# A hybrid decoder layer on one core: a third place for row tiles, one cast on VectorE, and other priorities for the scheduler

## The chip, the core and the metric

The kernel runs on one core of a Trainium2 chip. The metric is the device time in microseconds (us) of one execution; lower is better. The core has TensorE (matmul), VectorE, ScalarE and GpSimd (named DVE, ACT and POOL in the profile), and SyncE (SP), which here only issues DMA transfers.

## What is computed

One layer of a decoder on 2048 rows (positions) of width 1024, all in float32. Shapes: 8 heads of 64 with 2 key/value heads and a window of 128; the other half of the mixer is a gated convolution over three positions; the feed-forward width is 4096.

```python
def reference(x, attn_norm_g, w_in, q_norm_g, k_norm_g, sinks, conv_w,
              attn_out_g, conv_out_g, w_out, mlp_norm_g, w_up, w_down):
    for l in range(DEPTH):                      # DEPTH = 1
        h = rms_norm(x, attn_norm_g[l])
        z = h @ w_in[l]
        ...                                     # q, k, v, gate_b, gate_c, xc are columns of z
        q = rms_norm(q, q_norm_g[l])
        k = rms_norm(k, k_norm_g[l])
        y_attn = swa_sink_attention(q, k, v, sinks[l])
        y_conv = gate_b * short_conv(gate_c * xc, conv_w[l])
        y = jnp.concatenate([rms_norm(y_attn, attn_out_g[l]),
                             rms_norm(y_conv, conv_out_g[l])], axis=-1)
        x = x + y @ w_out[l]
        hm = rms_norm(x, mlp_norm_g[l])
        x = x + jnp.square(jax.nn.relu(hm @ w_up[l])) @ w_down[l]
    return x
```

## The kernel before

**Precision.** A float32 product is made of three matmuls: each operand is split into a high part (a cast on ScalarE) and a low part (value minus high part, on VectorE), and `mm3` (L271) adds high x high, high x low and low x high into one PSUM bank. Lines 273, 274 and 275 are these three.

**Stages.** The mixer part (to about 690 us) works through four chunks of 512 rows. The feed-forward part follows: the up product (`u`, L1430) and the down product (`d`, L1537), each in seven block products in Strassen's manner, with x rows and weights combined ahead of time.

**The first chunk** (`first_chunk`, L489, called L595) is issued by hand, in program order on every engine. Its first product goes through eight slices k of the width: `load_x0` and `load_w0` fetch them, `turn(k)` transposes the x slice on TensorE (`pt_a`), `split0(k)` splits the weights (`w_q`), `moved(k)` multiplies the transposed slice by the norm's gain and splits it into high and low (`h_a`, L515 and L516), and `product0(k)` runs 12 matmuls into four banks (`pz`). `spin(n)` issues matmuls of the identity whose result nobody reads, to have TensorE at work while the first data come in; `SPIN` holds two numbers of them. ScalarE's first work on data is the cast of `w_q` for k = 0 and then `h_a` for k = 0.

**The later order** is made by a scheduler that places the instructions of each engine by priority. Two generators are interleaved in each chunk. `mixers` (L1007) goes through the four blocks of 128 rows of the attention: scores (`psc`), softmax (`sc`), probabilities transposed (`ptp`), split into `pp` and masked on GpSimd (L734), the product with the values (`po`, L773), the result `o` on VectorE, the mean of its squares (`pa`, L794, a matmul with `mean`; `ms` is read from it by VectorE). `besides` (L963) yields the big matmuls one step at a time: the convolution's projections (`pc`, `px`, `pb`), the out projection (`pout`, with weights `w_wo` that come back from DRAM in two halves, high and low), the next chunk's rows (`xt_a`, scaled on VectorE in L289, transposed on TensorE) and the next chunk's projection (`pz`). Between the steps of the attention `fill(n)` takes n steps from `besides`; the numbers come from the table `FILL`, a row for each chunk. `ahead(i)` (L195) raises or lowers the priority of a step by column i of the table `PRIO`, a row for each chunk:

```python
def ahead(i):
    offset = PRIO[stage[0]][i]
    return tc.high_priority(offset=offset) if offset else nullcontext()
```

The columns: 0 q and k transposed, 1 softmax, 2 q and k normed, 3 `pa`, 4 values and probabilities, 5 `po`, 6 attention output, 7 split of weights, 8 scaling of rows, 9 transposes of rows, 10 convolution, 11 eviction of the out projection. `LATER` lowers the priority of writing split weights to DRAM.

**The end of chunk 3.** `prepare_mlp` (L929) prepares x for the up product. Eight row tiles (t, i) of 128 rows are fetched from DRAM (`xt_m`, `fetch`, L938), scaled on VectorE (L289), and transposed on TensorE in two groups of four (`raised`, L309, `pt_m`), which ScalarE copies into `xm`. Tiles with i = 0 are then written to DRAM (`x_put`, L340, `xop`); those with i = 1 also go through four subtractions on VectorE (`x_sums`, L354) and five writes. There are two places for fetched tiles, so a fetch on SP's queue waits until the tile two before it is transposed. All transposes of row tiles and `pa` go through one PSUM bank (`tr`). SP issues transfers in order: what stands behind a fetch that waits also waits. `xm` are two buffers that take the space of the chunk's `h` (high and low).

## Time and profile before

| what | value |
|---|---|
| three runs | 1925.79, 1926.3, 1927.85 us; median 1926.3 |
| the profiled execution | 1926.52 us, of which the span 1924.7 |
| TensorE | busy 1912.8 us (99% of the span), 8923 instructions |
| VectorE, ScalarE, GpSimd | busy 63%, 43%, 14% |
| chain that ended last | TensorE 90%, VectorE 6%, DMA 2%, issue 1% |
| DMA | 414.32 MB, 215 GB/s on average |

A busy time is the sum of the spans of an engine's instructions. Matmuls overlap, and their ends are modelled, so a TensorE that is busy is not yet one at its peak; the time from start to start of consecutive matmuls says more than their durations. An idle time is put down to what ended last before the instruction could start.

### The profile page before, as it was taken

The page shows a single profiled execution, that of the slowest core. Times are in us where ns is not written, and L with a number is a line of the kernel's source. Part 1 is how long each engine was busy: PE and PEld are TensorE (multiplying, and loading weights), DVE is VectorE, ACT ScalarE, POOL GpSimd, SP SyncE. Part 2 cuts the span into 40 slices and gives each one's busy share as a digit, 9 for nine tenths or more (in the row PEclk, how much of TensorE's full clock was granted, in tenths as well). Part 3 has the DMA queues.
Part 4 walks back from the last instruction along what each step waited for, and adds up shares of the span by engine and source line. Part 5 has one row for each costly group of instructions (what it writes and reads, how often), then busy time and mean ns, then how long its engine had stood idle before and what let it go on. Part 6 is the DMA issues. An engine that isn't in the chain of part 4 may idle for free.

```text
span 1924.7 us, 24566 instructions
## 1 busy us (share of the span) xinstructions
PE 1912.8 (99%) x8923; PEld 1589.3 (83%) x8923; DVE 1204.5 (63%) x1848; ACT 829.9 (43%) x1565; POOL 273.4 (14%) x477
## 2 busy tenths in 40 slices
PE   9999999999999999999999999999999999999999
PEld 8888888888888778888888888888888888888887
DVE  4885657447456769989887767666534334457531
ACT  5564434335344437454565555553432232232320
POOL 2122212302221112223110110101000000100000
PEclk9999999999999999999999999999999999999999
DMA  8984854463573797777665454437954457766631
GB/s 296 335 304 129 316 208 175 189 249 153 190 268 144 257 355 257 220 235 241 218 225 199 168 170 135 161 137 301 373 203 150 142 164 230 278 223 220 212 128 55
DMA packets 232792, 414.32 MB, mean 215 GB/s; under 512 B 51672, under 2 KB 136160, under 8 KB 219872
## 3 DMA queue, kind: packets, MB, share of 16 engines
q1 hardware_dynamic: 203840, 336.98, 51.9%
q0 software_dynamic: 15424, 51.40, 6.8%
q10 hardware_dynamic: 13408, 24.39, 3.4%
q8 instruction: 70, 1.15, 0.2%
q14 instruction: 50, 0.41, 0.1%
HBM read 286.87 MB, written 125.83 MB: 214 GB/s over the span
## 4 chain that ended last, share of the span: by engine, by line
PE 90%; DVE 6%; DMA 2%; issue 1%; ACT 1%; POOL 1%; ACTq 0%; SPq 0%; DVEq 0%; POOLq 0%
PE d L1537 32%; PE u L1430 29%; PE pout L273 3%; PE pout L275 3%; PE pout L274 3%; PE pz L273 2%; PE pz L274 2%; PE pz L275 2%; PE pc_c L273 1%; PE pc_c L275 1%; PE pc_c L274 1%; PE psc_b L685 1%; PE pz L523 1%; PE px_c L274 1%; PE px_c L273 1%; PE px_c L275 1%
## 5 line engine op out<-in xcount | busy, mean ns | idle before, releaser
L1430 PE MATMUL u<-op_x,wop 128*128 128x512 f32 x2688 | 610.3, 390 | 0.5 <-DVE wop L424 0.5
L1537 PE MATMUL d<-op_w,op_f 128*128 128x512 f32 x2688 | 609.4, 389 | 0.0
L1430 PEld LDWEIGHTS u<-op_x,wop 128*128 128x128 f32 x2688 | 504.5, 188 | 105.8 <-DVE wop L424 0.9
L1537 PEld LDWEIGHTS d<-op_w,op_f 128*128 128x128 f32 x2688 | 504.7, 188 | 104.6
L405 DVE TENSOR_TENSOR op_f<-op_f 128x1024 fp32r<-128x1024 f32 x112 | 136.9, 1224 | 232.4 <-ACT op_f L404 231.9
L404 ACT CAST op_f<-op_f 128x1024 fp32r<-128x1024 f32 x112 | 117.7, 1052 | 352.0 <-DMA op_f<-fop 344.9
L424 DVE TENSOR_TENSOR wop<-wu,wop 128x512 fp32r<-128x512 f32 x156 | 111.8, 718 | 35.0 <-DMA wu<-in_w_up_dram 17.6
L423 ACT CAST wop<-wu 128x512 fp32r<-128x512 f32 x156 | 95.9, 619 | 83.0 <-PE u L1430 79.1
L1166 POOL DMA_DIRECT2D fop<-s x96 | 51.9, 541 | 442.4 <-DVE s L1169 438.1
L1172 DVE TENSOR_TENSOR u<-u,u 128x512 f32<-128x512 f32 x128 | 87.7, 685 | 21.7 <-PE u L1430 21.7
L405 DVE TENSOR_TENSOR op_w<-raw,op_w 128x1024 fp32r<-128x1024 f32 x56 | 68.4, 1222 | 27.2 <-ACT op_w L404 27.0
L404 ACT CAST op_w<-raw 128x1024 fp32r<-128x1024 f32 x56 | 58.8, 1052 | 46.0 <-PE d L1537 23.4
L1178 ACT ACTIVATE u<-u 128x512 f32<-128x512 f32 x64 | 40.5, 633 | 73.1 <-DVE u L1172 71.2
L702 ACT ACTIVATE sc_b<-sc_b,ngm_b 128x128 f32<-128x128 f32 x128 | 49.6, 390 | 23.9 <-DVE ngm_b L699 23.9
L734 POOL TENSOR_SCALAR_AFFINE_SELECT pp_b<-pp_b 128x512 fp32r<-128x512 f32 x60 | 39.6, 673 | 112.6 <-ACT pp_b L727 59.8
L1379 POOL DMA_DIRECT2D wds<-raw x16 | 8.5, 534 | 327.8 <-DVE raw L1377 327.8
L423 ACT CAST wop<-wu_s 128x512 fp32r<-128x512 f32 x64 | 39.6, 620 | 31.0 <-PE u L1430 22.8
L273 PE MATMUL pout<-w_wo,yt_c 128*128 128x512 f32 x128 | 52.5, 410 | 0.0
L275 PE MATMUL pout<-w_wo,yt_c 128*128 128x512 f32 x128 | 52.1, 407 | 0.0
L424 DVE TENSOR_TENSOR wop<-wu_s,wop 128x512 fp32r<-128x512 f32 x64 | 44.6, 698 | 10.9 <-ACT wop L423 10.7
L274 PE MATMUL pout<-w_wo,yt_c 128*128 128x512 f32 x128 | 51.3, 400 | 0.0
L273 PE MATMUL pout<-w_wo,at_b 128*128 128x512 f32 x128 | 50.2, 395 | 0.0
(258 smaller groups left out, 3110.1 us busy)
## 6 DMA issues: line engine op xcount, KB each, us to landing
op_f<-fop SPq DMA_DIRECT2D x112, 512.0 KB, 4.3
raw<-in_w_down_dram SPq DMA_DIRECT2D x72, 512.0 KB, 4.3
wu<-in_w_up_dram SPq DMA_DIRECT2D x128, 256.0 KB, 4.0
w_wo<-wo SPq DMA_DIRECT2D x24, 1024.0 KB, 6.7
fop<-s POOLq DMA_DIRECT2D x96, 256.0 KB, 2.5
fop<-u ACTq DMA_DIRECT2D x64, 256.0 KB, 2.8
op_x<-xop SPq DMA_DIRECT2D x28, 512.0 KB, 6.7
w_q<-q SPq DMA_DIRECT2D x12, 1024.0 KB, 7.5
```

Of the source, the lines that this page charges most:

```text
L273: nc.tensor.matmul(ps, st(0), mv(0), start=first, stop=False)
L274: nc.tensor.matmul(ps, st(0), mv(1), start=False, stop=False)
L275: nc.tensor.matmul(ps, st(1), mv(0), start=False, stop=last)
L404: nc.scalar.copy(op[:, 0], raw)
L405: nc.vector.tensor_tensor(op[:, 1], raw, op[:, 0].bitcast(F32), op=ALU.subtract)
L423: splits.append(nc.scalar.copy(hi, blk).ins)
L424: nc.vector.tensor_tensor(lo, blk, hi.bitcast(F32), op=ALU.subtract)
L702: nc.scalar.activation(sc[:, hd, :], sc[:, hd, :], AF.Exp, bias=ngm[:, hd : hd + 1], accum_out=den[:, hd : hd + 1])
L1166: eng.dma_start(fop_dram[tb][ORDER_DOWN.index(i)][n // 2][:, n % 2], b)
L1172: return nc.vector.tensor_tensor(dst, ps, b, op=ALU.add).ins
L1430: nc.tensor.matmul(pt, wops[i][:, a, k, :], xops[tb, p][k // 2][:, b, k % 2, :], start=p not in GOES_ON and k + j == 0, stop=k + j == NB + ...
L1537: nc.tensor.matmul(ps[tb][j], fs[tb][:, a, k, j * P : (j + 1) * P], w[:, b, k, :], start=first and p not in GOES_ON and k + n == 0, stop=l ...
```

## The change

Four edits. The first product takes the high part of `h` for k = 0 from VectorE and no longer from ScalarE; one more idle matmul is issued behind the first transposes, and the second slice is transposed behind the first four products and no longer ahead of them. In `prepare_mlp` three tiles are fetched ahead; the third and sixth of them go into half of the second `xm` buffer (pieces 3 and 7), which is not in use until later. The tables `PRIO` and `FILL` get other numbers, and `LATER` falls from 250 to 190.

```diff
-SPIN = (5, 0)
+SPIN = (5, 1)
...
-    (40, 0, 160, -10, 10, 0, 10, 60, -20, 30, 0, 300),
+    (40, 0, 160, -10, 30, 0, 10, -10, -20, 30, 0, 300),
...
-    ((27, 6), (9, 9, 5, 6, 3), (6, 7, 8, 5, 5), (8, 13, 8, 7, 7), (10, 1, 9, 5, 0)),
+    ((27, 6), (9, 9, 5, 6, 3), (6, 7, 7, 5, 5), (8, 13, 8, 7, 7), (11, 1, 9, 3, 0)),
...
-                r = slice((NB * k + j) * P, (NB * k + j + 1) * P)
-                nc.tensor.transpose(pt[:, j * P : (j + 1) * P], xt[:, r], ident)
+                r = slice(j * P, (j + 1) * P)
+                nc.tensor.transpose(pt[:, r], xt[:, k, r], ident)
...
-            nc.scalar.activation(h[0][:, k], pt, AF.Copy, scale=g_in[k])
+            if k:
+                nc.scalar.activation(h[0][:, k], pt, AF.Copy, scale=g_in[k])
+            else:
+                nc.vector.tensor_scalar(h[0][:, k], pt, g_in[k], None, op0=ALU.mult)
...
         spin(SPIN[1])
-        turn(1)
...
-            split0(k)
-            moved(k)
+            if k:
+                split0(k)
+                moved(k)
+            else:
+                nc.scalar.copy(hl0[0][:, 0], by_k(raw0[0])[:, 0])
+                moved(0)
+                nc.vector.tensor_tensor(hl0[0][:, 1], by_k(raw0[0])[:, 0], hl0[0][:, 0].bitcast(F32), op=ALU.subtract)
...
-                product0(k, [(i, t) for i in range(3) for t in range(NT)])
+                for i in range(3):
+                    product0(k, [(i, t) for t in range(NT)])
+                    if not k and not i:
+                        turn(1)
...
-            def fetch(t, i):
+            halves = lambda w: w.rearrange("p (k c) -> p k c", k=2)
+
+            def fetch(n):
+                t, i = tiles[n]
                 r = i * CH + t * P
-                xts[t, i] = row("xt", f"xt_m{i}_{t}", 2)
-                nc.sync.dma_start(xts[t, i], x1_dram[r : r + P, :])
+                xt = xs[1][:, 3::4] if n % 3 == 2 else halves(row("xt", f"xt_m{i}_{t}", 2))
+                nc.sync.dma_start(xt, halves(x1_dram[r : r + P, :]))
                 with ahead(8):
-                    scaled(xts[t, i], rs_x1[:, r // P : r // P + 1], gb)
+                    scaled(xt, rs_x1[:, r // P : r // P + 1], halves(gb))
+                xts[t, i] = xt
...
-            fetch(*tiles[0])
-            fetch(*tiles[1])
+            for n in range(3):
+                fetch(n)
...
-                if n + 2 < len(tiles):
-                    fetch(*tiles[n + 2])
+                if n + 3 < len(tiles):
+                    fetch(n + 3)
```

In the tables the other changes are: `PRIO`, chunk 0: values and probabilities 10 to 30, split of weights 60 to -10 (the row shown); chunk 1: scaling of rows 50 to -40; chunk 2: attention output 260 to 120, eviction 10 to 0; chunk 3: `pa` -10 to 200. `FILL`: chunk 0, last block, one step less (5 to 4) ahead of the values; chunk 2, three fewer and one fewer; chunk 3 as shown.

What this does to the order, at three places. First VectorE at the start of the kernel, before and then after (`w_q_0` the weights of slice 0, `h_a_250` the high part of h, `h_a_251` the low part):

```order
L552 COPY g_in<-pg 128x8
L506 TENSOR_TENSOR w_q_0_242<-raw_q_240,w_q_0_242 128x512
L516 SCALAR_TENSOR_TENSOR h_a_251<-pt_a_0_290,g_in,h_a_250 128x512
L506 TENSOR_TENSOR w_q_1_243<-raw_q_240,w_q_1_243 128x512
L516 SCALAR_TENSOR_TENSOR h_a_251<-pt_a_1_295,g_in,h_a_250 128x512
```

```order
L555 COPY g_in<-pg 128x8
L518 TENSOR_SCALAR h_a_250<-pt_a_0_290,g_in 128x512
L519 SCALAR_TENSOR_TENSOR h_a_251<-pt_a_0_290,g_in,h_a_250 128x512
L566 TENSOR_TENSOR w_q_0_242<-raw_q_240,w_q_0_242 128x512
L506 TENSOR_TENSOR w_q_1_243<-raw_q_240,w_q_1_243 128x512
L519 SCALAR_TENSOR_TENSOR h_a_251<-pt_a_1_308,g_in,h_a_250 128x512
```

VectorE has one operation more, and the low part of h now stands ahead of the low part of the weights.

Second GpSimd in chunk 0, around the masking of the probabilities of block 1 (`pp_b_0` and `pp_b_1` are its two head groups; `ms_c` and `rc` the scale of the convolution's half, `ss_a` and `rs_a` that of a row tile of the next chunk), before and then after:

```order
L734 AFFINE_SELECT pp_b_0_1_1484<-pp_b_0_0_1483 128x512
L190 TENSOR_SCALAR ms_c_1536<-ms_c_1536 128x4
L191 TENSOR_TENSOR rc_659<-ms_c_1536,mhalf 128x4
L1000 TENSOR_TENSOR rc_659<-rc_659,rs_252 128x4
L190 TENSOR_SCALAR ss_a_2_1552<-ss_a_2_1552 128x1
L191 TENSOR_TENSOR rs_a_2_1554<-ss_a_2_1552,mhalf 128x1
L734 AFFINE_SELECT pp_b_0_1_1484<-pp_b_0_0_1483 128x512
L734 AFFINE_SELECT pp_b_1_1_1495<-pp_b_1_0_1494 128x512 x2
```

```order
L744 AFFINE_SELECT pp_b_0_1_1485<-pp_b_0_0_1484 128x512 x2
L190 TENSOR_SCALAR ms_c_1537<-ms_c_1537 128x4
L191 TENSOR_TENSOR rc_660<-ms_c_1537,mhalf 128x4
L1014 TENSOR_TENSOR rc_660<-rc_660,rs_252 128x4
L744 AFFINE_SELECT pp_b_1_1_1496<-pp_b_1_0_1495 128x512 x2
L190 TENSOR_SCALAR ss_a_2_1553<-ss_a_2_1553 128x1
```

Both masks of the first group now come ahead of the scale `rc`, and those of the second group ahead of `rs_a`.

Third SP's queue near the end of chunk 3 (`w_wo_0`, `w_wo_1` with 1662 or 1663 as their source are the high and low half of the weights of the last projection piece of the convolution's half; `xt_m` and `xm_6234` are fetches of row tiles), before and then after:

```order
L244 DMA w_wo_0_6453<-wo_0_1662 128x2048
L244 DMA w_wo_1_6454<-wo_1_1663 128x2048
L938 DMA xt_m_2_6266<-x_dram 128x1024
L340 DMA xop_0_76<-xm_6232 256x1x256
L340 DMA xop_1_77<-xm_6232 256x1x256
L938 DMA xt_m_3_6324<-x_dram 128x1024
```

```order
L951 DMA xm_6234<-x_dram 128x2x512
L244 DMA w_wo_0_6455<-wo_0_1663 128x2048
L951 DMA xt_m_3_6269<-x_dram 128x1024
L340 DMA xop_0_76<-xm_6233 256x1x256
L340 DMA xop_1_77<-xm_6233 256x1x256
L340 DMA xop_0_76<-xm_6233 256x1x256
L951 DMA xt_m_0_6327<-x_dram 128x1024
L340 DMA xop_1_77<-xm_6233 256x1x256
L340 DMA xop_0_76<-xm_6233 256x1x256
L951 DMA xm_6234<-x_dram 128x2x512
L340 DMA xop_1_77<-xm_6233 256x1x256
L340 DMA xop_0_76<-xm_6233 256x1x256
```

The third tile's fetch moved ahead of the weights' high half, and the low half (`w_wo_1`, row 176 of the queue before) is no longer behind the high half: it stands in row 189, after the fetches of tiles 3 to 6 as well. The first operand of the up product (`op_x`, L403) moved from row 189 to row 208, behind most writes of the last tile. On TensorE, in chunk 2, 42 rows stand between the last matmul of `po` of block 11 and its `pa` before, and 66 after.

## The prediction

> **What bounds the kernel now.** I read the page first, then what TensorE waits for, then the timeline around each wait.

> ```profile
> PE 1912.8 (99%) x8923; PEld 1589.3 (83%) x8923; DVE 1204.5 (63%) x1848; ACT 829.9 (43%) x1565; POOL 273.4 (14%) x477
> L1430 PE MATMUL u<-op_x,wop 128*128 128x512 f32 x2688 | 610.3, 390 | 0.5 <-DVE wop L424 0.5
> L1537 PE MATMUL d<-op_w,op_f 128*128 128x512 f32 x2688 | 609.4, 389 | 0.0
> ```

> TensorE is busy for 99% of 1924.7 us, and the 5376 matmuls of the two feed-forward products, 63% of the span, wait 0.5 us in all. 609.4 us over 2688 is 0.227 us a matmul (each lasts 0.39 us, but they overlap): that is the pace against which I measure holes. The change removes no matmul, so it can only win holes, and only ahead of 690 us. The view of waits, on TensorE alone, lists them:

> ```profile
> PE idle L547 <- POOL ident L170: 1.6, 1, 1.6
> PE po_b L773 <- POOL pp_b L734: 1.4, 3, 0.9
> PE pt_m L315 <- DVE xt_m L289: 1.4, 2, 1.1
> PE pa_b L794 <- DVE o_b L789: 0.8, 1, 0.8
> PE pt_m L315 <- DVE ms_b L796: 0.6, 1, 0.6
> PE u L1430 <- DVE wop L424: 0.5, 1, 0.5
> PE pz L523 <- ACT h_a L515: 0.4, 1, 0.4
> PE pt_a L511 <- DMA x<-in_x_dram: 0.2, 1, 0.2
> ```

> These eight, the largest, come to 6.9 us. The first is the launch and the sixth lies in the feed-forward part; neither is touched. So about 4.8 us of idle time can go. A hole costs a little more than its idle time, because TensorE's overlap has to start again; below I take start to start, less 0.23.

> **Part 1, the start** (h's high part on VectorE, one more idle product, four transposes moved behind the first four products). The timeline of before:

> ```profile
> 4.22 1.11 PE L511 MATMUL pt_a<-ident,x 128*128 128x128 f32 x4
> 5.57 1.12 PE L511 MATMUL pt_a<-ident,x 128*128 128x128 f32 x4 [0.24 <-DMA x<-in_x_dram]
> 5.86 0.62 ACT L505 CAST w_q<-raw_q 128x512 fp32r<-128x512 f32 x1 [2.52 <-DMA raw_q<-in_w_in_dram]
> 6.38 0.68 ACT L515 ACTIVATE h_a<-pt_a,g_in 128x512 fp32r<-128x512 f32 x1
> 6.51 0.69 DVE L506 TENSOR_TENSOR w_q<-raw_q,w_q 128x512 fp32r<-128x512 f32 x1 [2.02 <-ACT w_q L505]
> 7.11 4.88 PE L523 MATMUL pz<-w_q,h_a 128*128 128x512 f32 x12 [0.42 <-ACT h_a L515]
> 7.11 0.75 DVE L516 SCALAR_TENSOR_TENSOR h_a<-pt_a,g_in,h_a 128x512 fp32r<-128x512 f32 x1
> 11.84 0.60 PE L511 MATMUL pt_a<-ident,x 128*128 128x128 f32 x4
> ```

> ScalarE casts w (to 6.48) and then h (to 7.06), and the first product waits for both. No row shows VectorE writing h's high part; its neighbours there took 0.69 and 0.75. It can begin when the first transposes end, 5.33, so it is done by 6.1, and w becomes last: the first product starts near 6.53 instead of 7.11, 0.58 earlier. VectorE's h low then ends at 6.85 and w low at 7.6, ahead of the fifth product (6.53 + 4 x 0.43 = 8.2). But the second group of transposes, which stood in TensorE's wait, now stands in its stream: four took 1.12 here, some 0.9 of it before the next can start. 0.9 - 0.58 is +0.3; against it, products that start earlier have more of their dozen done when the clock rises. Bounds: -0.6 (the transposes cost nothing) and +0.9 (nothing won by the earlier start). I take **+0.1**. The extra idle product lies in a wait and costs nothing.

> How slow the start is, the rate shows:

> ```profile
> 7.10:8.90 1.80, 1.79 (x4) 1.00 1.04 389
> 11.84:14.60 2.76, 2.57 (x12) 1.00 0.96 342
> ```

> Four of 512 columns start in the first 1.8 us, 0.43 us apiece, yet the granted clock (after the counts) reads 1.00; the first twelve took 11.84 - 7.11 = 4.73 us, the next twelve 2.76 with their transposes. So the array is at half pace until about 11. [...]

> **Part 2, chunk 0** (values and probabilities earlier).

> ```profile
> 130.82 0.68 DVE L728 TENSOR_TENSOR pp_b<-ptp_b,pp_b 128x512 fp32r<-128x512 f32 x1
> 131.08 1.04 POOL L191 TENSOR_TENSOR rc<-ms_c,mhalf 128x4 f32<-128x4 f32 x1
> 132.72 0.40 PE L773 MATMUL po_b<-pp_b,vd 128*128 128x512 f32 x1
> 133.33 1.93 POOL L734 TENSOR_SCALAR_AFFINE_SELECT pp_b<-pp_b 128x512 fp32r<-128x512 f32 x3
> 134.02 0.50 PE L773 MATMUL po_b<-pp_b,vd 128*128 128x512 f32 x1 [0.90 <-POOL pp_b L734]
> ```

> The hole is 134.02 - 132.72 - 0.23 = 1.07 us: GpSimd masks the second half of head group 0 only at 133.33, after the chain for rc. In the new order VectorE splits both groups and GpSimd masks group 0 before that chain and group 1 behind it. I put the last mask, two of 0.64 (a third of 1.93) behind a chain that ends near 131.8, at 133.1 and TensorE's need at 133.6: the hole goes, with 0.5 us to spare. What pays: VectorE does those splits and other steps of 0.7 earlier, ahead of the scaling of the next chunk's first row tile, whose transposes then wait some 0.3 longer, while those of a later tile wait some 0.2 less. Bounds -1.4 (all holes here go) and +0.4 (two steps of 0.7 in front, hole gone). I take **-1.0**. Chunk 1 changes only a few rows, with one scaling later, close to its need: +0.1, between -0.4 and +0.5.

> **Part 3, chunk 2.**

> ```profile
> 539.39 0.39 PE L275 MATMUL pout<-w_wo,at_b 128*128 128x512 f32 x1
> 540.13 0.29 DVE L789 TENSOR_TENSOR o_b<-o_b 128x128 f32<-128x128 f32 x1
> 540.56 0.35 PE L794 MATMUL pa_b<-mean,o_b 128*128 128x1 f32 x2 [0.79 <-DVE o_b L789]
> ```

> A hole of 540.56 - 539.39 - 0.23 = 0.94 us: the mean of the squares of block 11 waits for VectorE. By the new order po_b11 moves up, and 66 matmuls instead of 42 stand between it and pa_b11, 24 more of 256 columns, by half of 0.23 about 2.7 us. VectorE needs the same time as before, so **-0.94**; ends -1.0 and 0 (its own queue is delayed as much).

> **Part 4, chunk 3** (the third place for x rows).

> ```profile
> 638.51 0.80 SPq L244 DMA_DIRECT2D w_wo<-wo  x2
> 661.55 1.28 DVE L289 SCALAR_TENSOR_TENSOR xt_m<-xt_m,rs_x,g_mlp 128x1024 f32<-128x1024 f32 x1 [1.15 <-DMA xt_m<-x_dram]
> 662.98 0.63 PE L315 MATMUL pt_m<-ident,xt_m 128*128 128x128 f32 x4 [1.09 <-DVE xt_m L289]
> 675.80 1.28 DVE L728 TENSOR_TENSOR pp_b<-ptp_b,pp_b 128x512 fp32r<-128x512 f32 x2
> 675.94 0.66 PE L315 MATMUL pt_m<-ident,xt_m 128*128 128x128 f32 x4 [0.60 <-DVE ms_b L796]
> 677.51 0.51 PE L773 MATMUL po_b<-pp_b,vd 128*128 128x512 f32 x1 [0.21 <-POOL pp_b L734]
> 679.25 0.50 PE L773 MATMUL po_b<-pp_b,vd 128*128 128x512 f32 x1 [0.33 <-POOL pp_b L734]
> DMA to landing us min/median/max: 4.7/6.7/8.5
> DMA to landing us min/median/max: 3.2/4.4/8.1
> ```

> (The last two rows are those of w_wo's loads in this window, and of xt_m.) A row tile is fetched only when the transposes of the tile two before it are done; landing (4.4) and scaling (1.28) then decide. With three places the fetch comes one tile earlier. The waits on xt_m (1.4 idle), on ms_b (0.6) and on pp_b (0.54), five holes, go as holes: 2.5 idle plus some 0.17 each to restart is 3.4. Three things take part of it back. First, SP: the low half of the weights of the last projection piece (w_wo, second of the pair at 638.51) moves from in front of all fetches to behind five of them, each waiting for transposes; I follow the order to an issue at about 655 and, with 6.7, a landing at 662, where TensorE wants it at 661 to 661.5: +0.5 to 1. Second, block 15's probabilities stay behind the sums of the row tiles on VectorE, and one bank holds all these transposes: +0.6. Third, the first operand of the up product is now loaded behind the last tile's sums instead of at 658: its split (VectorE, two of 1.22, then 0.7) can end up to 1 us behind TensorE. Together I take +1.5 of 3.4, **-1.9**; ends -4 (nothing new waits) and +1 (all three at their worst, 4.4).

> Sum: 0.1 - 1.0 + 0.1 - 0.94 - 1.9 = -3.64. The profiled run took 1926.52 us (1.8 outside its span), 0.22 above the median, so 1922.9 for it and **1922.6** in terms of the median. A difference of 0.2%, 3.85 us, is about what a measurement can tell from none; the forecast falls just short of it, and its own range, 1920.6 to 1924.6, holds both.

> **Rivals.**
> (a) Everything clears. Part 4 gives -4 and part 2 -1.4, the rest as above: 0.1 - 1.4 + 0.1 - 0.94 - 4 = -6.1, 1920.2. For it: the three repayments each hang on less than 1 us. Against: SP issues in order, and five fetches are ahead of the weights.
> [...]
> (c) Chunk 3 gains nothing, since what was gained on row tiles is waited for on weights and operand: 0 instead of -1.9, 1924.5.
> (d) Slower: the weights' low half lands too late. Every fetch ahead of it on SP waits for a place, so one slow landing (8.1, shown above) at the second and fifth tile shifts it by 3.7 each; with 8.5 for its own, 1.8 more, it lands 9.2 late. TensorE then stands at the projection, since its stream has nothing else in front; the first repayment of 0.5 to 1 becomes 9.7, behind which the others hide: some 8 more, and -3.6 + 8 is +4.4, 1930.7. It decides from a landing near 669.5, where the sum is +3.85. For it: 0.91 of the DMA engines' time is used in this stretch:

> ```profile
> 638.00:690.00 52.00, 49.42 (x258) 38.87 (x257) 39.87 (x64) 22.86 (x41) 9.70 (x14) 1.00 0.91 290
> ```

> Against it: two of eight or more landings would both have to be the worst.

> **How the numbers follow.** Chances: forecast 0.48 (half of it beyond 0.2%), (a) 0.2, (b) 0.08, (c) 0.12, (d) 0.12. Faster is 0.24 + 0.2, and a little of (c) where the other parts do better: 0.46. Slower is (d) and the worst ends of (b) and (c): 0.15. Same is 0.39. The range of 8 in 10 runs from (a) less a start that wins 0.6, 1919.3, to the near end of (d), 1928.5, with the most of (d) left out above.

> **What would show it.** Right: no wait of po_b on pp_b near 133, none of pa_b near 540, first product at 6.5 and the third group of transposes near 11.9; no wait of pt_m on xt_m, and w_wo's last load issued at 655 and landed at 662; u starting near 686.5, all of it shifted by the same amount from there to the end. Wrong: a wait of pout on a DMA of over 2 us after 660, the first twelve products taking 7 us, or new holes in chunk 1.

## The result, and the profile after

| | before | changed |
|---|---|---|
| first comparison, 22 runs each | 1926.6 us median (1924.02 to 1928.76) | 1923.53 (1920.87 to 1927.77) |
| second, 27 and 11 runs | 1927.26 (1924.16 to 1931.43) | 1923.83 (1921.52 to 1925.87) |

The ratio is 0.9983 with a 95% interval of 0.9977 to 0.999, and 0.9985 (0.9976 to 0.9994) in the second: 3.1 to 3.4 us faster, just short of the 0.2% named in the prediction. Forecast were 1922.6 and -3.64.

What TensorE waits for in the changed kernel (engine, line, releaser; total, times, longest):

```profile
PE pout L274 <- DMA w_wo<-wo: 2.2, 2, 1.9
PE idle L550 <- POOL ident L170: 1.6, 1, 1.6
PE po_b L783 <- POOL pp_b L744: 0.7, 1, 0.7
PE pz L526 <- ACT w_q L564: 0.5, 1, 0.5
PE pa_b L804 <- DVE o_b L799: 0.3, 1, 0.3
```

The waits on the row tiles (`xt_m`, 1.4) and on `pa`'s reader `ms_b` (0.6) are gone; those on `pp_b` and `o_b` are down to half or less and stand in other places (675 and 622 us, where it was 134 and 540); at the head stands a wait that was not there, of the last projection piece on its weights. The time by stages, from the starts of TensorE's matmuls in the timeline of two profiles of each kernel (the second of each was taken among the experiments):

| stage, from start to start | before | before again | changed | changed again |
|---|---|---|---|---|
| launch to the last of the 96 first products | 33.60 | 31.22 | 33.19 | 33.77 |
| chunk 0, to the 96th matmul of its out projection | 120.53 | 121.80 | 118.76 | 118.75 |
| to the 145th matmul of chunk 1's out projection | 222.06 | 222.06 | 221.96 | 222.04 |
| over chunk 2, to the first `pb` matmul of chunk 3 | 208.47 | 208.47 | 207.66 | 207.70 |
| to the up product's first matmul | 105.43 | 105.02 | 107.47 | 105.39 |
| up product, its first 1344 matmuls | 316.29 | 315.52 | 316.35 | 316.29 |

(Where an expectation below counts from the last convolution product of chunk 3, it is this `pb` matmul.) Chunk 2 gives 0.8 and chunk 0 gives 1.8 or 3.1; chunk 3, forecast at -1.9, loses 0 to 2.4. In chunk 0 the hole of 1.07 on `pp_b` was the largest; the changed kernel at that place (`ssc` is the sum of squares of the convolution's half, from which `rc` is made):

```profile
125.25 0.68 DVE L875 TENSOR_TENSOR ssc<-ssc,y_c 128x512 f32<-128x512 f32 x1
129.57 1.38 POOL L191 TENSOR_TENSOR rc<-ms_c,mhalf 128x4 f32<-128x4 f32 x1
131.18 1.23 POOL L744 TENSOR_SCALAR_AFFINE_SELECT pp_b<-pp_b 128x512 fp32r<-128x512 f32 x2
132.61 0.71 PE L783 MATMUL po_b<-pp_b,vd 128*128 128x512 f32 x2
```

The last two masks are done at 132.41, before TensorE wants them at 132.61. The timeline of TensorE at the end of chunk 3 in the changed kernel:

```profile
658.32 0.47 PE L273 MATMUL pout<-w_wo,yt_c 128*128 128x512 f32 x1
658.80 0.66 PE L315 MATMUL pt_m<-ident,xt_m 128*128 128x128 f32 x4
659.21 0.71 PE L783 MATMUL po_b<-pp_b,vz 128*128 128x512 f32 x2
661.84 0.55 PE L274 MATMUL pout<-w_wo,yt_c 128*128 128x512 f32 x1 [1.92 <-DMA w_wo<-wo]
662.18 0.63 PE L275 MATMUL pout<-w_wo,yt_c 128*128 128x512 f32 x1
662.61 0.63 PE L273 MATMUL pout<-w_wo,yt_c 128*128 128x512 f32 x1
...
665.17 0.58 PE L273 MATMUL pout<-w_wo,yt_c 128*128 128x512 f32 x1
665.59 0.39 PE L274 MATMUL pout<-w_wo,yt_c 128*128 128x512 f32 x1
665.82 0.39 PE L275 MATMUL pout<-w_wo,yt_c 128*128 128x512 f32 x1
```

L274 is the first product that needs the weights' low half. It waits 1.92, a hole of 661.84 - 659.52 - 0.23 = 2.09 (the second `po_b` started at 659.52). Behind it nine products start 0.43 apart instead of 0.23, until 665.6. The windows of the same stretch (length, busy and count, granted clock, DMA share, GB/s) show why:

```profile
659.80:661.80 2.00, 0.12 (x1) 1.00 0.97 347
661.80:665.40 3.60, 3.56 (x9) 0.55 1.08 375
665.40:669.00 3.60, 3.60 (x16) 0.98 0.21 74
```

Over the 3.6 us behind the hole the granted clock reads 0.55. The hole cost 2.09, and the slow clock behind it some 1.7 more. The load itself, on SP's queue:

```profile
636.82 0.59 SPq L244 DMA_DIRECT2D w_wo<-wo  x1
...
652.23 0.41 SPq L951 DMA_DIRECT2D xt_m<-x_dram  x1
652.85 0.51 SPq L340 DMA_DIRECT2D xop<-xm  x1
653.41 0.60 SPq L244 DMA_DIRECT2D w_wo<-wo  x1
```

The high half is issued at 636.82, the low half at 653.41, and the traced landing is at 661.80, 8.4 us later.

### The profile page after: what moved, and what is told of

The parts are those of the page before. It is cut to its first block, busy times and chain, and to the rows that moved or that the text cites. A ratio compares the mean times of both kernels' runs of the same rounds, so it can differ in the third digit from the quotient of the medians.

```text
span 1923.8 us, 24574 instructions
## 1 busy us (share of the span) xinstructions
PE 1913.5 (99%) x8925; PEld 1591.4 (83%) x8925; DVE 1206.1 (63%) x1849; ACT 830.6 (43%) x1564; POOL 275.8 (14%) x477
## 3 DMA queue, kind: packets, MB, share of 16 engines
q8 instruction: 70, 1.15, 0.2%
## 4 chain that ended last, share of the span: by engine, by line
PE 65%; DMA 1%; SPq 0%; POOL 0%; DVE 0%; ACT 0%; issue 0%; POOLq 0%
PE d L1551 32%; PE u L1444 31%; DMA w_wo<-wo 1%; PE pout L274 1%; PE pout L275 1%; PE pout L273 0%; PE pt_m L315 0%; SPq L244 0%; PE po_b L783 0%; POOL pp_b L744 0%; DVE d L1497 0%; ACT xm L316 0%; SPq L340 0%; SPq L418 0%; PE pa_b L804 0%
## 5 line engine op out<-in xcount | busy, mean ns | idle before, releaser
L1551 PE MATMUL d<-op_w,op_f 128*128 128x512 f32 x2688 | 609.4, 389 | 0.0
L424 DVE TENSOR_TENSOR wop<-wu,wop 128x512 fp32r<-128x512 f32 x156 | 111.5, 716 | 36.2 <-ACT wop L423 18.4
L274 PE MATMUL pout<-w_wo,yt_c 128*128 128x512 f32 x128 | 51.5, 402 | 1.9 <-DMA w_wo<-wo 1.9
L275 PE MATMUL pout<-w_wo,yt_c 128*128 128x512 f32 x128 | 52.5, 410 | 0.0
L424 DVE TENSOR_TENSOR wop<-wu_s,wop 128x512 fp32r<-128x512 f32 x64 | 44.5, 697 | 11.0 <-ACT wop L423 10.8
```

The lines of the kernel that those rows point to most:

```text
L274: nc.tensor.matmul(ps, st(0), mv(1), start=False, stop=False)
L275: nc.tensor.matmul(ps, st(1), mv(0), start=False, stop=last)
L424: nc.vector.tensor_tensor(lo, blk, hi.bitcast(F32), op=ALU.subtract)
L1551: nc.tensor.matmul(ps[tb][j], fs[tb][:, a, k, j * P : (j + 1) * P], w[:, b, k, :], start=first and p not in GOES_ON and k + n == 0, stop=l ...
```

## The experiments

Theory 1: the third place itself gains in chunk 3, and the weights' low half, which it pushes behind the fetches, takes it back. Theory 2: the third place crowds the end of chunk 3 whatever the weights do. Stages are those of the table.

**again**: the changed kernel unaltered.

> The changed kernel as it is, for a second profile and times beside the next two. If the loss at the end of chunk 3 belongs to the order of SP's queue, the wait of the last projection piece for the low half of its weights comes again (1 to 3 us, its load issued near 653 and landing near 660 to 663), and about 3.5 us of products at half pace behind it whenever the wait is near 2 us. If it was an accident of one run, there is no such wait here. Total 1921 to 1926.

The weights were issued at 653.98 and landed at 662.01; the wait came again, with a hole of 1.29, and the clock did not fall. The first profile's half pace is not in every run; the wait is in all six profiles with this order of SP (holes of 1.3 to 2.1, the load taking 8.0 to 8.5 each time).

**weights_early**: the weights of that piece raised in priority.

```diff
-                hl = ahead_parts.pop((half, dh), None) or out_weights(c, half, dh)
+                with tc.high_priority(offset=400) if half and dh and c + 1 == NCHUNK else nullcontext():
+                    hl = ahead_parts.pop((half, dh), None) or out_weights(c, half, dh)
```

> The changed kernel, with only the load of the last projection piece's weights (half 1, second column half, chunk 3) raised in priority, so that both halves stand on SP ahead of the third tile's fetch, as in the kernel before. Theory 1, the weights behind five fetches are the cost: no wait of pout on w_wo after 650, no half pace there, the up product starts 3 to 4 us earlier than in the changed kernel's first profile (near 685.5 instead of 689.0), time 1919 to 1921, that is 2 to 4 below the changed kernel. Theory 2, the third place itself crowds the end of chunk 3 (fetches, one PSUM bank, VectorE): the wait goes, others come, the up product starts at 688 to 689.5 and the time is that of the changed kernel within 1 us.

SP's queue and TensorE's waits (largest three):

```profile
636.67 0.80 SPq L244 DMA_DIRECT2D w_wo<-wo  x2
637.51 0.56 SPq L952 DMA_DIRECT2D xm<-x_dram  x1
```

```profile
PE idle L550 <- POOL ident L170: 1.6, 1, 1.6
PE u L1445 <- DVE wop L424: 0.8, 1, 0.8
PE pz L526 <- DVE h_a L518: 0.5, 1, 0.5
```

Both halves land by 643.91, the wait on w_wo and the half pace are gone. The stage to the up product takes 103.75 us, 1.6 and 3.7 below the two profiles of the changed kernel and 1.3 to 1.7 below the kernel before. In its place stands the wait of `u` on its operands, a hole of 0.97. Theory 1 holds by the stages. The total is 1922.88 (ratio to before 0.9983, 0.9974 to 0.9991) beside 1923.83 in the same comparison: 1 us lower, which the intervals do not separate; the expected 2 to 4 did not show in it.

**early_again** is the same kernel later, beside early_spin3 below.

> The kernel with early weights and one idle product again, beside the one with three: runs spread over 1919.5 to 1926, median near 1922.5; no wait of pout on w_wo near 660; from the last convolution product of chunk 3 (its first matmul) to the first of the up product 103.5 to 104.3 us, against 105.44 in the kernel before and 107.47 and 105.39 in the two profiles of the changed kernel.

The stage took 103.68. Median 1921.92, ratio 0.9981 (0.9972 to 0.999). Here the start of the up product gave back more: a hole of 0.81 on its operands and one of 1.28 for the next weights, 317.88 for its first 1344 matmuls against 316.3.

**no_third**: two places, everything else new.

```diff
-            for n in range(3):
-                fetch(n)
+            fetch(*tiles[0])
+            fetch(*tiles[1])
```

(and the rest of `prepare_mlp` and `raised` as before.)

> The changed kernel with two places for row tiles, as before; start, priorities and filling steps are the new ones. Theory 1: chunks 0 to 2 gain their 3 us as in the changed kernel; chunk 3 has the waits on xt_m, ms_b and pp_b of the kernel before again (about 3.4 us of holes), no wait on w_wo, so the up product starts near 687 and the time is 1922.5 to 1924, about that of the changed kernel. Theory 2: it is faster than the changed kernel by 2 us or more.

```profile
PE pt_m L315 <- DVE xt_m L289: 2.6, 3, 1.8
PE idle L550 <- POOL ident L170: 1.6, 1, 1.6
PE pout L273 <- DMA w_wo<-wo: 0.8, 1, 0.8
```

(The wait on `w_wo` here is one for the next weights, at 690.8 us.) The waits on the row tiles are back, larger than before (a hole of 1.93), and the stage takes 106.46; its median is 1926.03, 2.2 above the changed kernel in the same comparison, 2.0 above the upper end that theory 1 expected, and the contrary of theory 2. By the stage the third place gains nothing sure with late weights (105.4 to 107.5 in the two profiles, against 106.46 without it) and 2.7 with early ones; the stages do not explain the 2.2 of the medians. The stage is also 1.0 to 1.4 longer than in the kernel before, which has two places as well: the new numbers for chunk 3 (`pa` and the filling steps) cost that much by themselves in this profile.

**third_alone**: the kernel before with the third place only.

> The kernel before with the third place alone. Both theories: the start and chunks 0 to 2 stand as before (first product at 7.1, hole at 133, hole at 540). Theory 1: the load of the weights' low half moves behind five fetches here too (so the order says), with a wait of 1 to 3 us; the up product starts between 689 and 692.

As expected in chunk 3 (the start was at full pace, with the first product at 6.72): weights issued at 655.27, landed at 663.61, a hole of 1.99, nine products at half pace, the up product at 690.51; one run of 1927.32. The order of SP comes from the third place and not from the tables.

**undo_p4** and **undo_p7_fill** take back two parts of the tables each.

```diff
-    (40, 0, 160, -10, 30, 0, 10, -10, -20, 30, 0, 300),
+    (40, 0, 160, -10, 10, 0, 10, -10, -20, 30, 0, 300),
...
-    (200, 0, 10, -50, 40, 0, 120, -20, 70, 280, 200, 0),
+    (200, 0, 10, -50, 40, 0, 260, -20, 70, 280, 200, 0),
```

> The changed kernel with two priorities back at their old values: chunk 0, values and probabilities (30 to 10), and chunk 2, attention output (120 to 260). The order of GpSimd in chunk 0 stays new (both masks of the first group ahead of rc, those of the second behind it), but the transposes of the probabilities go back among the projection's products. If the order on GpSimd removed the hole near 132, there is no hole of po_b on pp_b there (under 0.3 us); if it was the earlier transposes and splits, a hole of 0.5 to 1.1 us comes back. Chunk 2: no hole near 540, since the number of matmuls between po_b11 and pa_b11 (67) stays.

No hole near 130, chunk 0 in 118.89 against 118.76: the early transposes, which stand among the projection's products again here, are worth nothing that can be seen. No hole of `pa` near 540; one run of 1924.01.

```diff
-    (40, 0, 160, -10, 30, 0, 10, -10, -20, 30, 0, 300),
+    (40, 0, 160, -10, 30, 0, 10, 60, -20, 30, 0, 300),
...
-    ((20, 17), (9, 16, 11, 9, 1), (9, 5, 11, 7, 2), (16, 8, 15, 6, 6), (9, 15, 11, 5, 2)),
+    ((20, 17), (9, 16, 11, 9, 1), (9, 5, 11, 7, 2), (16, 8, 15, 6, 9), (9, 15, 11, 5, 3)),
```

> The changed kernel with the priority of the weights' split in chunk 0 back at 60 and the filling steps of chunk 2 back at their old values. Chunk 0: the transposes stay early and the masks of both groups stand ahead of rc, no hole on pp_b near 132. Chunk 2: 43 matmuls between po_b11 and pa_b11 again, so the hole of 0.9 us of pa_b on o_b near 540 comes back.

```profile
130.06 2.44 DVE L256 SCALAR_TENSOR_TENSOR w_wo<-raw_wo,g_y,w_wo 128x512 fp32r<-128x512 f32 x3
131.93 1.48 POOL L191 TENSOR_TENSOR rc<-ms_c,mhalf 128x4 f32<-128x4 f32 x1
133.38 0.64 POOL L744 TENSOR_SCALAR_AFFINE_SELECT pp_b<-pp_b 128x512 fp32r<-128x512 f32 x1
134.07 0.50 PE L783 MATMUL po_b<-pp_b,vd 128*128 128x512 f32 x1 [0.70 <-POOL pp_b L744]
539.65 0.39 PE L275 MATMUL pout<-w_wo,at_b 128*128 128x512 f32 x1
540.84 0.35 PE L804 MATMUL pa_b<-mean,o_b 128*128 128x1 f32 x2 [0.80 <-DVE o_b L799]
```

Chunk 2 as expected: the hole near 540 is back, 0.96. Chunk 0 against the expectation: holes of 0.87 (`po_b`) and 0.85 (row tile), the stage back at 120.68; one run of 1929.07. The gain of chunk 0 hangs on one number, the priority of the weights' split. With that number at 60, VectorE has its old order there: a split of the weights at 116.21 stands ahead of the row maxima (in the changed kernel at 117.92, behind them), and of the three `ssc` the second ends at 124.83 and the last at 127.88, against 119.34 and 125.93 in the changed kernel (125.06 and 128.19 before). GpSimd begins the chain for `rc` at 130.24, against 128.82 there and 130.34 before, and the last mask is late again. A mask of the second group stands behind `rc` here, which the expectation overlooked; in the changed kernel both do, and there the chain ends early enough.

**early_pa**: early weights, and `pa` in chunk 3 back at -10.

> The kernel with the weights loaded early, and the priority of pa in chunk 3 back at -10 as before the change. The new hole of pa_b13 near 622 (0.48 us) goes; no wait of pout on w_wo near 660. By theory 1 the up product starts 0.3 to 0.8 us earlier than in the kernel with early weights alone, measured from the last convolution product of chunk 3; time 0 to 1 us lower, which the totals cannot tell. If the new place of pa only moves the wait, no difference.

The hole near 622 went, and one of 1.92 came near 665, where a row tile's transposes wait for ScalarE's copy: the stage takes 104.32 against 103.75. The wait moved. Median 1922.2, ratio 0.9972 (0.9961 to 0.9982).

**spin3** and **early_spin3**: three idle products instead of one, on early_pa and on weights_early.

```diff
-SPIN = (5, 1)
+SPIN = (5, 3)
```

> The kernel above with three idle products instead of one behind the first transposes, so that TensorE has no gap of 0.5 us ahead of the first product. If the clock gate counts these idle products as work, the array is at full pace from the first product on more often: the first dozen then takes 3.6 us and not 5.5, and the median falls by up to 2 us. If the phase of the gate's window decides alone, the time is the same within 0.5 us, or 0.1 to 0.3 higher for the idle products.

> The kernel with early weights (pa left at the new priority) and three idle products behind the first transposes instead of one. Three profiles of kernels with one idle product began at half pace (first dozen 5.5 to 5.9 us) and two at full pace; the one with three idle products at full pace. If idle products decide, this kernel begins at full pace (first dozen with the transposes in it 3.6 to 3.7 us), its runs lie within 2.5 us of one another, near 1920 to 1921.5, and its median is 1 to 2 below the next kernel's. If only the phase of the gate's window decides, both kernels spread over 4 to 5 us alike, with medians within 0.7.

spin3 began at full pace, 1921.57 in five runs (1920.23 to 1922.29), ratio 0.9965 (0.9952 to 0.9978); early_spin3 left half pace at 7.7, and its ten runs spread over 1920.13 to 1924.61 with a median of 1921.92, that of early_again to the hundredth. The five near one another had been chance, and in the totals the idle products decide nothing that can be seen. In the start of this pair they do: by the record of the granted clock early_spin3 went to full pace at 7.71 and early_again at 11.17, and their first products end at 32.01 and 33.61 (the last section says why these two can be compared). The window in the two expectations is, so far as the runs show it, the step of 3.413 us in that section. In all, the four versions with early weights had medians of 1921.6 to 1922.9 in three comparisons, where the changed kernel had 1923.5 and 1923.8 in two. All are faster than the kernel before beside them, with ratios of 0.9965 to 0.9983; the changed kernel has 0.9983 and 0.9985, and only weights_early stood beside it. So that early weights beat the changed kernel too is likely by the stages but not shown by the totals.

**turn_back**: the second slice's transposes ahead of the first product again.

```diff
         spin(SPIN[1])
+        turn(1)
...
-                    if not k and not i:
-                        turn(1)
```

> The changed kernel with the second slice's transposes ahead of the first product again, h's high part still on VectorE. They wait for x (5.57 before) and take 0.9 to 1.1, so the first product cannot start before 6.6 to 6.7. If the transposes among the first products are paid for by the earlier start, as the prediction has it, the second dozen starts within 0.4 us of the changed kernel's at the same pace: at half pace 11.5 to 12.3, at full pace 9.5 to 10. If transposes there hold the clock back, this kernel leaves half pace 1 us or more earlier, counted from its first product (4.0 us in the kernel before and in the changed kernel).

```profile
6.09 1.12 PE L511 MATMUL pt_a<-ident,x 128*128 128x128 f32 x4 [0.34 <-DMA x<-in_x_dram]
6.86 4.50 PE L526 MATMUL pz<-w_q,h_a 128*128 128x512 f32 x12
11.21 0.60 PE L511 MATMUL pt_a<-ident,x 128*128 128x128 f32 x4
```

First product at 6.86, second dozen at 11.56, full pace from 10.10 on, 3.2 us after the first product: between the expected cases, and within the scatter of the other starts, so it does not decide between them; one run of 1925.83.

**before_again**: the kernel before, a second profile.

> The kernel before, for a second profile. By the stages of the first profiles the changed kernel wins 0.4 at the start, 1.8 in chunk 0 and 0.8 in chunk 2 and loses 1.1 to 2 in chunk 3, which is less in sum than the medians' 3.1. If the first profile of the kernel before was a lucky one at the end of chunk 3, this one takes 106 to 108 us from the last convolution product to the up product, where that took 105.44. If not, it takes 105 to 105.8 again, and the rest of the difference lies in how often the two kernels begin at half pace.

The stage to the up product took 105.02: the first profile was not a lucky one there. It was lucky in chunk 0. This run (1924.24) began at full pace, 2.4 us earlier at the end of the first products, and 1.3 of that was lost near 118:

```profile
6.56 3.04 PE L523 MATMUL pz<-w_q,h_a 128*128 128x512 f32 x12 [0.23 <-ACT h_a L515]
118.15 0.40 PE L275 MATMUL pb_c<-h_a,w_wb 128*128 128x512 f32 x1
119.88 0.66 PE L301 MATMUL pt_a<-ident,xt_a 128*128 128x128 f32 x4 [1.32 <-DVE ms_b L796]
```

In the first profile TensorE came 2.3 us later to the same place, and the hole was 0.28. VectorE sets the pace there in the kernel before: it comes to `ms_b` 1.97 us after TensorE's `pa` here, and 0.81 after it in no_third, which also began at full pace. Two splits of weights (0.74 each) stand in its queue ahead, one of which the changed kernel does later, with the squares `ssc` in its place, though still ahead of `ms_b`; and TensorE's transposes that need the bank come eight matmuls behind `pa` there, and three before. third_alone, also begun at full pace, has the same hole, 1.59; no_third, spin3 and undo_p4, with the new priority and a full pace, have none. In undo_p7_fill both engines have the old order there again, so it too comes from the split's number; that run began at half pace and could not show the hole.

## Why the prediction was right, and where its steps were not

The time, the sign and the range held. The sum, -3.64 against -3.1 to -3.4, was right by two errors that offset each other, in chunk 0 and in chunk 3; that it came so near is luck.

- **Part 1, start, +0.1.** The first product came at 6.26 to 6.47 in five profiles of the changed start at half pace (6.53 forecast; 6.82 in a sixth, where the weights landed late), the third transposes at 11.43 and 12.01 (11.9). The first products end at 33.19 to 33.77, before 33.60; among runs at full pace at 31.31 and 31.34 (31.84 where the weights landed late), before and in third_alone at 31.22 and 31.37. So 0.1 with a scatter of 0.4 fits. The cast's 0.58 is right where the weights land last: the first product starts 0.67 after the beginning of ScalarE's cast of `w_q` in the changed kernel (5.63 and 6.30), and 1.26 after it before (5.30 and 6.56 in the second profile). At full pace no_third starts 0.29 ahead of the second profile of before (6.27 and 6.56) and ends 0.12 behind it (31.34 and 31.22): what the cast gains, the transposes take.
- **Part 2, chunk 0, -1.0.** Measured -1.8, and -3.1 where the run starts at full pace. The hole on `pp_b` went as forecast, but the named cause, the transposes and masks moved ahead, was wrong in part: undo_p4 moved the transposes back and lost nothing. The step that failed is "what pays: VectorE does those splits earlier": VectorE was relieved, of a split of the weights that it now does later, so that the squares and with them GpSimd's chain for `rc` came earlier (its end 131.23, against 132.40 before and 131.8 in the prediction). The -10 for these splits stood in the diff and was given no price. The waits on row tiles, forecast at +0.3 and -0.2, both went (0.28 and 0.24 before; 1.49 for the first where the start is fast). Chunk 1, +0.1, was 0.0 to -0.1.
- **Part 3, chunk 2, -0.94.** The hole went and came back with the filling steps; of it 0.35 returned further down, where a product of the out projection waits for VectorE (for `ms_b` in one profile, for `x` in the other). Measured -0.8.
- **Part 4, chunk 3, -1.9.** Measured 0 to +2.4. The gain on the tiles is there (weights_early, -1.3 to -1.7 to the up product's first matmul), and the first repayment is the one forecast, mis-sized: a landing at 662 was right (661.80, 662.01), with 653.4 + 8.4 instead of 655 + 6.7, but TensorE wanted it at 659.75 and 660.77 and not at 661 to 661.5, so the hole was 1.3 to 2.1 and not 0.5 to 1. The half pace behind it had no term, nor had the new numbers for chunk 3, which cost 1.0 to 1.4 in no_third. The second was 0.85 (0.6 forecast); of the third, up to 1, the changed kernel paid 0.3 to 0.4 as a wait for the next weights, and the versions with early weights 0.3 to 1.0 on the operands.
- **Rivals.** (d) had the right mechanism; with both unlucky fetches it needed a landing 9 us late, and there was none in six profiles. (c) is nearest for chunk 3. For (b), with its chance of 0.08, no run shows that transposes among the first products make the clock rise later: half pace lasted 3.9 and 4.8 us after the first product in the changed kernel, 4.1 and nothing in the kernel before, 3.2 in turn_back. A dozen more at half pace would have cost 1.9, by the kernel before: 5.08 from the first product to the second dozen's start, and 3.19 from there to the third's. In its second profile, with the same code, the first of these took 3.23, so the pace of the start differs from run to run without any change to the transposes; in two profiles of the changed kernel the first dozen and its transposes took 5.48 and 5.89 (6.30 to 11.78, 6.47 to 12.36), not the 7 named as a sign against the forecast.

What stays open: which share of the runs begins at half pace in each kernel, since only profiles show it (9 of 14 did), and so how much of the medians' 3.1 is chunk 0 at either pace. The profiles alone do not add up to 3.1: at half pace those of the changed kernel are 0.9 and 2.6 shorter than the one of the kernel before, and at full pace the changed kernel was not seen. `LATER`, the new numbers of chunk 1 and the eviction in chunk 2 were not taken back one by one.

## What to carry to other kernels

An extra buffer lets fetches be issued earlier, and in a queue that issues in order, as SP's did here, whatever is issued earlier puts something else later (the weights' low half, issued at 653.41, where the kernel before issued it with the high half at 638.51): look up what lost its place, when TensorE wants it, and follow TensorE's new stream to that point with its gains counted in. Price every number of a priority table that lowers work on an engine near the path, since here one such number carried most of the gain. Where runs differ by more than the change, compare stages of several profiles rather than two totals.

## What the runs showed of the hardware that was not expected

```profile
658.75:662.16 3.41, 1.48 (x8) 1.00 0.97 316
662.16:665.57 3.41, 3.41 (x9) 0.50 1.06 367
659.79:663.20 3.41, 2.29 (x12) 1.00 1.02 374
663.20:666.61 3.41, 3.41 (x17) 1.00 0.97 337
660.80:664.21 3.41, 1.82 (x13) 1.00 1.10 337
```

TensorE was busy for 1.46 (turn_back), 1.48 (the changed kernel) and 1.58 us (third_alone) in the three steps behind which the clock fell, and for 2.29 and 1.82 in the two shown that hold most of a hole and were not followed by half pace. But at the end of its work the changed kernel has a step of 1.54 (1918.26 to 1921.67), and the granted clock reads 1.00 behind it (1921.67 to 1923.80). So neither the length of a hole nor the busy time of a step separates all of these cases, and what decides no run shows.

- **2.4 us won at the start are not always won.** In the kernel before 1.3 of them were lost at 118 us to VectorE, in the changed order none (no_third, spin3 and undo_p4): by these profiles the change is worth 1.3 more when the start is fast.
